# Three pairs of feed-forward groups as seven block products each, in a two-block transformer kernel

## The chip, the core and the metric

The kernel runs on one core of a Trainium2 chip as a single launch. The metric is the device time of that launch in microseconds (us); smaller is better. TensorE is called PE in the rows, VectorE DVE, ScalarE ACT, GpSimd POOL and SyncE SP; PEld is TensorE's loading of the stationary operand.

## What is computed

Two blocks of two layers each run over 256 tokens of width 1024. Every layer has a feed-forward, a token mixer and a second feed-forward, so there are eight feed-forwards, and the change touches these alone. Cut to what matters:

```python
D_MODEL, SEQ, D_FF = 1024, 256, 2816

def swiglu(x, w13, w2):                      # first block
    a, b = jnp.split(x @ w13, 2, axis=-1)    # w13: 1024 x 5632
    return (jax.nn.silu(a) * b) @ w2         # w2: 2816 x 1024

x = layer_norm(ALPHA * x + 0.5 * swiglu(x, ffn1_w13[l], ffn1_w2[l]), ln_g[l, 0], ln_b[l, 0])
m = mixer(x, ...)
x = layer_norm(ALPHA * x + m, ln_g[l, 1], ln_b[l, 1])
x = layer_norm(ALPHA * x + 0.5 * swiglu(x, ffn2_w13[l], ffn2_w2[l]), ln_g[l, 2], ln_b[l, 2])
# second block: the same swiglu with rms_norm around it, x = x + 0.5 * rms_norm(h, gain)
```

All of it is float32. A product of two float32 matrices is made of three TensorE products in a reduced type: each operand is split into a high part (a rounding copy) and a low part (the difference), and high times high, high times low and low times high are summed in PSUM.

## The kernel before

The tokens are two halves of 128 rows, i = 0 and 1. Weights come in units of 128x1024 float32 (512 KB), one DMA each, in the exact order in which they are used (the host lays them out so; `fetch`, line 215, issues on SP's queue into `stg`, 4 buffers). `split` (line 257) makes of each unit the high part `wh` on ScalarE (line 267) and the low part `wl` on VectorE (line 273), in two halves of 512 columns. `wh` and `wl` are tiles of one ring, `whp`, of 24 tiles, so 12 split units at most stand ahead of TensorE. All other work tiles of 128x512 float32 (activations, normalisation rows, hidden parts) share one pool `sp` of 31 slots.

A feed-forward (`ffn`, line 376) has 66 units: 11 groups of 4 units for the first product and 22 rows of one unit for the second. A group `g` is 256 columns of the gate and 256 of the up part; for each token half it is 24 matmuls of 128x128 by 128x512 into one PSUM bank of the pool `grp` (4 banks). `hidden` (line 395) takes the bank: Silu on ScalarE, product on VectorE, then two clock steps later two transposes on TensorE and a high and a low part `hT`. A row is 12 matmuls for both halves into the accumulators `accs` (pool `big`, 4 banks). The first two groups (`OWN`) run by each token half on its own, since the halves arrive at different times from the layer before; then `joint` (line 417) runs both halves on each unit, in the order of the tuple `FFN` (line 57); the last six rows run by each half again.

The order of work is set in two ways. `run_all` writes the program with a counted clock (`later(n, fn)` puts `fn` n steps on, a joint unit counts two steps), and SP and POOL run exactly in that order. TensorE, VectorE and ScalarE are put in order by a planner, which plays the program through with its own costs, takes ready instructions by program order, and hands out ring tiles and slots as they come free in its plan; on the chip each engine then runs that fixed list. `mm3` (line 297, matmuls on line 301) is the helper behind nearly all matmuls, `transposed` (line 282, line 285) the one behind all transposes. `to_x` (line 303) turns the layer's input into `xh` and `xl`, the stationary parts of the next feed-forward or mixer.

In four of the eight feed-forwards POOL multiplies norm gains in advance: `pre_gains` (line 451, 4 operations) in the second feed-forward of the first block's second layer, and `gains` (line 510, 6 operations) in three of the second block's four. They use rows that SP loads in the middle of the weight stream (`prepare`, line 361).

Before the change the tuple `FFN` has no entry of kind "s", so `made` is None for every unit, and `operand` and the lists of products stand unused.

## Time and profile before

| | us |
|---|---|
| median of 3 runs | 2211.48 (2207.61 to 2212.41) |
| the profiled execution | 2206.83 |
| its span in the trace | 2205.1 |
| TensorE busy | 2169.9 (98% of the span) |
| VectorE busy | 1456.1 (66%) |
| ScalarE busy | 1173.5 (53%) |
| GpSimd busy | 271.5 (12%) |
| granted TensorE clock | 0.997 of full speed |

The span is the profiled execution without some 1.7 us around it. Matmuls overlap: one shows 0.39 us, but they follow each other at a shorter pitch, so the pitch is read from runs of many, not from the mean of one. The same holds for VectorE and ScalarE back to back.

### The profile page before, as it was taken

Reading aid. Unit: us, or ns where it says so; the run is one execution under the profiler, and the core shown is the slowest. Engines: PE = TensorE matmul, PEld = TensorE weight load, DVE = VectorE, ACT = ScalarE, POOL = GpSimd, SP = SyncE. Lnnn points to the kernel's source line nnn. Section 1 sums busy time; section 2 is a strip of 40 time slices with the busy share of each in tenths; the row PEclk is TensorE's granted clock in tenths of the full one; section 3 lists DMA queues with packets and bytes.
Section 4 is the critical chain, followed back from the end, with each engine's and each line's share of the span. In section 5 each row is a group of like instructions: output and inputs, shape, how many; then the busy total and the mean of one; then the engine's idle time right before and its main releaser. Section 6 shows DMA issues by size and latency. Waiting matters only on the chain.

```text
span 2205.1 us, 29139 instructions
## 1 busy us (share of the span) xinstructions
PE 2169.9 (98%) x10256; PEld 1791.8 (81%) x10256; DVE 1456.1 (66%) x2653; ACT 1173.5 (53%) x2339; POOL 271.5 (12%) x319
## 2 busy tenths in 40 slices
PE   8999999999999999999999999999999999999998
PEld 6888888888888888888878887788888888788887
DVE  6656787655755679666584668676657466877463
ACT  6544755544544475554554554665446355566352
POOL 0000420000000033001001004610100100650000
PEclk9999999999999999999999999999999999999999
DMA  7855455655565445565645643537555474345561
GB/s 275 271 189 158 148 182 175 223 196 189 182 205 188 156 158 181 180 203 191 210 157 196 218 145 120 172 102 238 182 190 177 157 236 149 114 134 167 177 219 49
DMA packets 115299, 394.59 MB, mean 179 GB/s; under 512 B 12880, under 2 KB 15312, under 8 KB 115152
## 3 DMA queue, kind: packets, MB, share of 16 engines
q1 hardware_dynamic: 115152, 392.73, 53.8%
q8 instruction: 80, 1.31, 0.2%
q14 instruction: 67, 0.55, 0.1%
HBM read 391.63 MB, written 1.05 MB: 178 GB/s over the span
## 4 chain that ended last, share of the span: by engine, by line
PE 88%; DVE 5%; ACT 2%; DMA 2%; POOL 2%; issue 1%; SPq 0%; DVEq 0%; POOLq 0%; ACTq 0%
PE g L301 54%; PE big L301 26%; PE g L285 3%; DMA stg<-in_ws_dram 2%; DVE wl L273 2%; ACT wh L267 1%; PE big L1150 1%; PE big L1179 1%; PE big L680 1%; DVE x L481 0%; DVE t L480 0%; PE big L1097 0%; POOL cu L1023 0%; PE big L882 0%; POOL qk L1024 0%
## 5 line engine op out<-in xcount | busy, mean ns | idle before, releaser
L273 DVE TENSOR_TENSOR wl<-stg,wh 128x512 fp32r<-128x512 f32 x1410 | 952.0, 708 | 506.7 <-ACT wh L267 498.5
L267 ACT ACTIVATE wh<-stg 128x512 fp32r<-128x512 f32 x1424 | 831.5, 625 | 622.7 <-PE g L301 313.6
L301 PE MATMUL g<-wh,xh 128*128 128x512 f32 x1952 | 783.0, 401 | 11.5 <-ACT wh L267 6.9
L301 PE MATMUL g<-wl,xh 128*128 128x512 f32 x1952 | 763.5, 391 | 0.0
L301 PE MATMUL g<-wh,xl 128*128 128x512 f32 x1952 | 762.6, 392 | 0.0
L301 PEld LDWEIGHTS g<-wh,xh 128*128 128x128 f32 x1952 | 368.4, 189 | 89.1 <-ACT xh L308 8.1
L301 PEld LDWEIGHTS g<-wh,xl 128*128 128x128 f32 x1952 | 367.9, 188 | 80.2 <-DVE xl L309 1.4
L301 PEld LDWEIGHTS g<-wl,xh 128*128 128x128 f32 x1952 | 368.6, 189 | 70.9 <-DVE wl L273 0.4
L301 PE MATMUL big<-wh,hT 128*128 128x512 f32 x1408 | 392.1, 391 | 0.0
L301 PEld LDWEIGHTS big<-wh,hT 128*128 128x128 f32 x1408 | 262.6, 188 | 53.6
L301 PE MATMUL big<-wl,hT 128*128 128x512 f32 x704 | 222.3, 390 | 0.0
L301 PEld LDWEIGHTS big<-wl,hT 128*128 128x128 f32 x704 | 132.2, 188 | 27.9
L373 POOL TENSOR_TENSOR m<-m,nhalf 128x1 f32<-128x1 f32 (+1 forms) x24 | 23.1, 964 | 848.3 <-DVE m L372 848.3
L507 POOL TENSOR_TENSOR m<-m,nhalf 128x1 f32<-128x1 f32 x24 | 15.3, 638 | 639.6 <-DVE m L506 639.6
L411 DVE TENSOR_TENSOR hT<-g,hT 128x256 fp32r<-128x256 f32 x176 | 68.2, 419 | 32.6 <-ACT hT L410 32.5
L410 ACT ACTIVATE hT<-g 128x256 fp32r<-128x256 f32 x176 | 59.3, 375 | 54.3 <-PE g L285 53.9
L400 ACT ACTIVATE sg<-g,m 128x256 f32<-128x256 f32 x88 | 41.0, 466 | 87.2 <-PE g L301 87.0
L405 DVE TENSOR_TENSOR sg<-g,sg 128x256 f32<-128x256 f32 x88 | 37.1, 421 | 69.1 <-ACT sg L400 67.0
L400 ACT ACTIVATE sg<-g 128x256 f32<-128x256 f32 x88 | 33.2, 377 | 54.9 <-PE g L301 54.9
L285 PE MATMUL g<-con,sg 128*128 128x128 f32 x352 | 57.4, 273 | 3.4 <-DVE sg L405 2.0
L285 PEld LDWEIGHTS g<-con,sg 128*128 128x128 f32 x352 | 43.7, 140 | 20.6 <-PE g L285 3.7
L402 DVE SCALAR_TENSOR_TENSOR sg<-g,sg 128x256 f32<-128x256 f32 x88 | 37.1, 421 | 30.2 <-ACT sg L400 28.9
(273 smaller groups left out, 1669.6 us busy)
## 6 DMA issues: line engine op xcount, KB each, us to landing
stg<-in_ws_dram SPq DMA_DIRECT2D x711, 512.0 KB, 4.0
row<-in_norm_gain_dram SPq DMA_DIRECT2D x24, 256.0 KB, 5.5
row<-in_ln_g_dram SPq DMA_DIRECT2D x12, 256.0 KB, 5.2
row<-in_ln_b_dram SPq DMA_DIRECT2D x12, 256.0 KB, 6.4
xT<-in_xT_dram SPq DMA_DIRECT2D x4, 256.0 KB, 6.4
x<-in_x_dram SPq DMA_DIRECT2D x4, 256.0 KB, 5.8
out_dram<-x SPq DMA_DIRECT2D x4, 256.0 KB, 2.0
con<-in_con_dram SPq DMA_DIRECT2D x1, 528.0 KB, 6.1
```

Of the source, the lines that this page charges most:

```text
L267: r = self.nc.scalar.activation(hi[:, c], w[:, c], AF.Copy)
L273: self.nc.vector.tensor_sub(lo[:, c], w[:, c], hi[:, c])
L285: self.nc.tensor.transpose(tp[:, hs(j)], src[:, hs(j)], self.ident)
L301: self.nc.tensor.matmul(accs[c], a, b[c], start=start and q == 0, stop=stop and q == 2)
L373: self.nc.gpsimd.tensor_tensor(out, out, self.nhalf[:, 0:n], op=ALU.pow)
L400: nc.scalar.activation(sg[:, 0:256], acc[:, 0:256], AF.Silu, scale=1.0 if rs is None else rs)
L402: nc.vector.scalar_tensor_tensor(sg[:, 256:512], acc[:, 256:512], 0.5, sg[:, 0:256], op0=ALU.mult, op1=ALU.mult)
L405: nc.vector.tensor_mul(sg[:, 256:512], acc[:, 256:512], sg[:, 0:256])
L410: nc.scalar.activation(t[:, 0:256], tp[:, 0:256], AF.Copy)
L411: nc.vector.tensor_sub(t[:, 256:512], tp[:, 0:256], t[:, 0:256])
L680: nc.tensor.matmul(ps[:, 64 * h:64 * h + 64].rearrange("p (c m) -> p c m", m=m), Z[:, hs(h)], view(Z[:, hs(h)], m)[:, :, 1, :], start=True ...
L1150: nc.tensor.matmul(ps[:, hh * S + j * P:hh * S + j * P + P], J["aq", i][r, hs(head // 2)], J["ak", j][r, hs(head // 2)], start=True, stop= ...
```

## The change

In each feed-forward three pairs of neighbouring groups (2 and 3, 4 and 5, 6 and 7) are computed in another way. A pair is a product of X (256 tokens by 1024) with W (1024 by 512 gate and 512 up columns), taken as 2 by 2 blocks: token halves by halves of the inner dimension, and halves of the inner dimension by gate or up. The eight block products become seven (Strassen's scheme in its form with 15 sums, the signs put into the X sums). A block product is 12 matmuls of 512 columns.

- `sums` makes four sums of X blocks on VectorE and splits them (four high copies on ScalarE, four differences on VectorE); for that `to_x` keeps float32 copies `A` of the transposed input by four more ScalarE copies per feed-forward. The parts take eight slots until the last pair is done.
- The four W blocks are loaded as before, 8 units per pair, but into tiles of the ring `whp`. Three products use them as they are in part: p1, p2, q5 and p3 each have a load of their own; q5, p6, p7 and q4 are made by one `tensor_add` of 128x1024 on VectorE per unit, in place. All 14 units of a pair are split, each by one ScalarE copy and one VectorE difference of 128x1024.
- `pair` runs the products in PSUM: p1, p6, p7 and q4 accumulate in one bank, and `keep` copies the bank out by ScalarE after p1, p6 and p7; q5 and p3 share another, copied after q5; p2 has a third. Three `tensor_add` and two products on VectorE and two Silu on ScalarE make the two hidden parts of 512 columns, each transposed by four transposes.
- The order: two own groups, then group 8, pair 2, group 9, pair 4, group 10, pair 6, rows 8, 9, 20, 21, and the last six rows 10 to 15. Inside a pair one row of the second product stands after p1, q5, p6 and p7. A feed-forward has 84 split units from the same 66 loads.

```diff
-FFN = (("g", 2), ("g", 3), ("r", 0, 8), ("g", 4), ("g", 5), ("g", 6), ("g", 7), ("r", 8, 16),
-       ("g", 8), ("g", 9), ("g", 10))
-LAST = (16, 17, 18, 19, 20, 21)
-PRODUCTS = ("p1", "q5", "p6", "p3", "p7", "p2", "q4")
-NEEDS = dict(p1="11", q5="12", p6="22", p2="21")
+FFN = (("g", 8), ("s", 2, 0, 1, 2, 3), ("g", 9), ("s", 4, 16, 17, 4, 5), ("g", 10), ("s", 6, 6, 7, 18, 19),
+       ("r", 8), ("r", 9), ("r", 20), ("r", 21))
+LAST = (10, 11, 12, 13, 14, 15)
+PRODUCTS = ("p1", "p2", "q5", "p3", "p6", "p7", "q4")
+LOADS = dict(p1="11", p2="21", q5="12", p3="22")
+BLOCKS = ("11", "21", "12", "22")
+GAPS = ("p1", "q5", "p6", "p7")
...
     def fetch(self, v):
         while self.next_dma <= min(v, self.nunit - 1):
             made = self.made[self.next_dma]
-            if made is None:
+            if not self.product(self.next_dma):
                 t = self.stages[self.next_dma] = self.stg.tile([P, 1024], F32, tag="stg", name=self.nm("stg"))
-            elif made[0] in NEEDS:
-                t = self.raw[NEEDS[made[0]], made[1]] = self.whp.tile([P, 1024], F32, tag="w", name=self.nm("raw"))
-            else:
-                t = None
-            if t is not None:
-                for c in (slice(0, 512), slice(512, 1024)) if self.next_raw == 0 else (slice(0, 1024),):
-                    self.nc.sync.dma_start(t[:, c], self.a["ws"][self.next_raw][:, c])
-                self.next_raw += 1
+                for c in (slice(0, 512), slice(512, 1024)) if self.next_dma == 0 else (slice(0, 1024),):
+                    self.nc.sync.dma_start(t[:, c], self.a["ws"][made][:, c])
+            elif made[0] in LOADS:
+                t = self.raw[made[:2]] = self.whp.tile([P, 1024], F32, tag="w", name=self.nm("raw"))
+                self.nc.sync.dma_start(t, self.block(LOADS[made[0]], *made[1:]))
             self.next_dma += 1
...
+    def block(self, b, u, base):
+        return self.a["ws"][base + 2 * BLOCKS.index(b) + u]
+    def operand(self, p, u, base):
 
 
         raw, add = self.raw, self.nc.vector.tensor_add
-        if p == "p1":
-            return raw["11", u]
-        if p == "q5":
-            t = raw.pop(("11", u))
-            add(t, t, raw["12", u])
-            raw["t1", u] = t
+        if p in ("q5", "p6"):
+            t = raw["p1", u]
+            add(t, t, raw["q5" if p == "q5" else "p3", u])
             return t
-        if p == "p6":
-            t = raw["t2", u] = self.whp.tile([P, 1024], F32, tag="w", name=self.nm("sum"))
-            add(t, raw.pop(("t1", u)), raw["22", u])
+        if p == "p7":
+            t = raw.pop(("p3", u))
+            add(t, t, raw.pop(("q5", u)))
             return t
-        if p == "p3":
-            return raw["22", u]
-        if p == "p7":
-            t = raw.pop(("12", u))
-            add(t, t, raw.pop(("22", u)))
+        if p == "q4":
+            t = raw.pop(("p1", u))
+            add(t, t, raw.pop(("p2", u)))
             return t
-        if p == "p2":
-            return raw["21", u]
-        t = raw.pop(("t2", u))
-        add(t, t, raw.pop(("21", u)))
-        return t
+        return raw[p, u]
...
-            w = self.stages.pop(v) if made is None else self.operand(*made)
+            product = self.product(v)
+            w = self.operand(*made) if product else self.stages.pop(v)
             hi = self.whp.tile([P, 1024], F32R, tag="w", name=self.nm("wh"))
             lo = self.whp.tile([P, 1024], F32R, tag="w", name=self.nm("wl"))
             halves = [slice(0, 512), slice(512, 1024)]
-            for h, c in enumerate(halves if made is None else [slice(0, 1024)]):
+            for h, c in enumerate([slice(0, 1024)] if product else halves):
...
-    def to_x(self, i, srcs):
-
+    def to_x(self, i, srcs, keep=False):
+        tps = []
         for h, src in enumerate(srcs):
             tp = self.transposed(src)
             hi, lo = (t[:, i, 512 * h:512 * h + 512] for t in (self.xh, self.xl))
             self.nc.scalar.activation(hi, tp, AF.Copy)
             self.nc.vector.tensor_sub(lo, tp, hi)
+            tps.append(tp)
+        if keep:
+            for h, tp in enumerate(tps):
+                t = self.sh["A", i, h] = self.slot(name="A")
+                self.nc.scalar.activation(t, tp, AF.Copy)
...
+    def sums(self, X):
+        nc = self.nc
+        for p, i, h in (("p1", 0, 0), ("p2", 0, 1), ("q4", 1, 1)):
+            X[p] = tuple(t[:, i, 512 * h:512 * h + 512] for t in (self.xh, self.xl))
+        a11, a12, a21, a22 = (self.sh.pop(("A", i, h)) for i in range(2) for h in range(2))
+        minus = lambda t, a, b: nc.vector.scalar_tensor_tensor(t, a, -1.0, b, op0=ALU.mult, op1=ALU.subtract)
+        def parts(p, t):
+            hi, lo = self.slot((P, 512), F32R, "Xh"), self.slot((P, 512), F32R, "Xl")
+            nc.scalar.activation(hi, t, AF.Copy)
+            nc.vector.tensor_sub(lo, t, hi)
+            X[p] = hi, lo
+        nc.vector.tensor_sub(a22, a22, a21)
+        nc.vector.tensor_sub(a21, a11, a21)
+        yield 1
+        parts("q5", a22)
+        yield 1
+        minus(a11, a22, a11)
+        yield 1
+        minus(a12, a11, a12)
+        yield 1
+        parts("p3", a12)
+        yield 1
+        parts("p6", a11)
+        yield 1
+        parts("p7", a21)
...
+        if i == 1:
+            J["X"] = {}
+            self.later(2, lambda: self.start(self.sums(J["X"])))
...
+        for what, n, *ks in FFN:
+            if what == "s":
+                yield from self.pair(J, n, ks)
...
+    def on(self, J, k):
+        wh, wl = self.units[self.pos[1]]
+        for i in range(2):
+            xh, xl = J["h", i, k]
+            self.mm3(J["accs", i], xh, xl, wh, wl, k == 0, False)
+        self.both(1)
+        yield
+    def pair(self, J, g, ks):
+        nc = self.nc
+        first = dict(p1="p1", p2="p2", q5="q5", p3="q5", p6="p1", p7="p1", q4="p1")
+        bank, kept, sg = {}, {}, {}
+        rows = dict(zip(GAPS[len(GAPS) - len(ks):], ks))
+        def keep(p):
+            t = kept[p] = self.slot(name="k" + p)
+            nc.scalar.activation(t, bank[p], AF.Copy)
+        def add(t, other):
+            nc.vector.tensor_add(t, t, other)
+        def silu(out, src, i):
+            rs = J["rs", i]
+            nc.scalar.activation(out, src, AF.Silu, scale=1.0 if rs is None else rs)
+        def hidden(i, t, sg):
+            nc.vector.scalar_tensor_tensor(t, t, -0.5 if J["rs", i] is None else -1.0, sg,
+                                           op0=ALU.mult, op1=ALU.mult)
+            def turn():
+                hi, lo = self.to_T(t, "hT")
+                for c in range(4):
+                    J["h", i, 2 * g + c] = hi[:, hs(c)], lo[:, hs(c)]
+            self.later(2, turn)
+        def after(p):
+            if p in ("p1", "q5", "p6", "p7"):
+                keep(p)
+            if p == "p2":
+                t = sg[0] = kept.pop("p1")
+                add(t, bank[p])
+                silu(t, t, 0)
+            elif p == "p6":
+                t = kept.pop("p6")
+                add(t, bank["p3"])
+                hidden(0, t, sg.pop(0))
+            elif p == "p7":
+                add(kept["p7"], kept.pop("q5"))
+            elif p == "q4":
+                t = self.slot(name="sg")
+                silu(t, bank[p], 1)
+                hidden(1, kept.pop("p7"), t)
+        for p in PRODUCTS:
+            bank[p] = self.bank(self.grp, "g") if first[p] == p else bank[first[p]]
+            xh, xl = J["X"][p]
+            for u in range(2):
+                wh, wl = self.units[self.pos[1]]
+                for j in range(2):
+                    k = 2 * u + j
+                    for q, (x, w) in enumerate(((xh, wh), (xh, wl), (xl, wh))):
+                        nc.tensor.matmul(bank[p], x[:, hs(k)], w[j], start=first[p] == p and k + q == 0,
+                                         stop=k == 3 and q == 2, skip_group_check=True)
+                for i in range(2):
+                    self.pos[i] += 1
+                if u:
+                    after(p)
+                yield
+            if p in rows:
+                yield from self.on(J, rows[p])
...
+    out, n = list(range(4 * OWN)), 4 * OWN
+    for what, _, *ks in FFN:
         if what == "s":
-            out += [(p, u) for p in PRODUCTS for u in range(2)]
+            base, gaps = n, GAPS[len(GAPS) - len(ks):]
+            n += 8
+            for p in PRODUCTS:
+                out += [(p, u, base) for u in range(2)]
+                if p in gaps:
+                    out.append(n)
+                    n += 1
         else:
-            out += [None] * (4 if what == "g" else at[1] - at[0])
-    return out + [None] * len(LAST)
+            m = 4 if what == "g" else 1
+            out += range(n, n + m)
+            n += m
+    return out + list(range(n, n + len(LAST)))
```

## Rows read from the trace of the kernel before

**Rows 1.** Page, busy time: engine, us, share of span, instructions.

```profile
span 2205.1 us, 29139 instructions
...
PE 2169.9 (98%) x10256; PEld 1791.8 (81%) x10256; DVE 1456.1 (66%) x2653; ACT 1173.5 (53%) x2339; POOL 271.5 (12%) x319
```

**Rows 2.** Chain that ended last, 460 to 520 us: start, length, what, count.

```profile
464.49 10.94 PE g L301 x48
475.43 0.44 PE g L285 x4
...
498.62 19.09 PE big L301 x84
```

**Rows 3.** Groups by line and shape, whole span: busy us, mean ns, idle before.

```profile
L273 DVE TENSOR_TENSOR wl<-stg,wh 128x512 fp32r<-128x512 f32 x1410 | 952.0, 708 | 506.7 <-ACT wh L267 498.5 <-PE g L285 3.4 <-PE g L301 0.7
...
L411 DVE TENSOR_TENSOR hT<-g,hT 128x256 fp32r<-128x256 f32 x176 | 68.2, 419 | 32.6 <-ACT hT L410 32.5
...
L471 DVE SCALAR_TENSOR_TENSOR t<-x,big 128x512 f32<-128x512 f32 x24 | 16.1, 683 | 15.8 <-PE big L301 15.8
...
L827 DVE TENSOR_TENSOR y<-y,y 128x512 f32<-128x512 f32 x8 | 5.5, 689 | 0.1
...
L813 ACT ACTIVATE b<-g 128x512 f32<-128x512 f32 x8 | 4.7, 591 | 2.2 <-PE g L301 2.2
```

**Rows 4.** Timeline, VectorE and ScalarE runs back to back: start, length, instruction, count.

```profile
14.28 5.13 DVE L273 TENSOR_TENSOR wl<-stg,wh 128x512 fp32r<-128x512 f32 x8 [0.17 <-ACT wh L267]
...
51.26 3.69 DVE L273 TENSOR_TENSOR wl<-stg,wh 128x512 fp32r<-128x512 f32 x6
...
1559.25 0.76 DVE L411 TENSOR_TENSOR hT<-g,hT 128x256 fp32r<-128x256 f32 x2 [2.43 <-ACT hT L410]
...
25.78 2.72 ACT L267 ACTIVATE wh<-stg 128x512 fp32r<-128x512 f32 x5
...
1558.83 0.66 ACT L410 ACTIVATE hT<-g 128x256 fp32r<-128x256 f32 x2 [2.46 <-PE g L285]
```

**Rows 5.** Waits, whole span: who for whom, us in total, times, longest.

```profile
DVE wl L273 <- ACT wh L267: 498.5, 422, 4.0
ACT wh L267 <- PE g L301: 313.6, 269, 2.8
...
POOL gr L458 <- PE big L301: 61.3, 1, 61.3
```

**Rows 6.** Windows: stretch, length, busy PE, PEld, DVE, ACT, POOL, clock, DMA share, GB/s.

```profile
381.00:409.00 28.00, 27.50 (x127) 22.31 (x128) 23.92 (x44) 17.23 (x34) 1.00 (x1) 1.00 0.60 203
...
1524.00:1545.00 21.00, 21.00 (x96) 17.39 (x95) 11.74 (x18) 9.10 (x18) 2.60 (x2) 1.00 0.68 233
1545.00:1568.00 23.00, 23.00 (x105) 19.00 (x104) 8.12 (x11) 4.93 (x12) 6.73 (x5) 1.00 0.14 46
1568.00:1592.00 24.00, 24.00 (x111) 19.86 (x110) 19.57 (x36) 17.31 (x35) 0.00 (x0) 1.00 0.84 283
```

**Rows 7.** Timeline, 1540 to 1556 us: POOL, VectorE, ScalarE around the gains.

```profile
1542.40 1.29 POOL L519 TENSOR_TENSOR xg<-x,row 128x512 f32<-128x512 f32 x1 [53.58 <-PE big L301]
...
1548.75 2.99 POOL L519 TENSOR_TENSOR xg<-x,row 128x512 f32<-128x512 f32 x2
...
1542.50 6.83 DVE L273 TENSOR_TENSOR wl<-stg,wh 128x512 fp32r<-128x512 f32 x4 [1.43 <-ACT wh L267]
...
1554.53 0.47 ACT L400 ACTIVATE sg<-g,m 128x256 f32<-128x256 f32 x1 [8.82 <-PE g L301]
```

**Rows 8.** Line 267 from 0 to 1544.97 and to 1567.6 us: high halves begun (xN).

```profile
L267 ACT ACTIVATE wh<-stg x1027: 612/630/657, 4.7 to 1544.6; 128x512 fp32r<-128x512 f32 x172
...
L267 ACT ACTIVATE wh<-stg x1031: 612/629/657, 4.7 to 1566.8; 128x512 fp32r<-128x512 f32 x172
```

**Rows 9.** Chain that ended last, whole span: end of eight rows, start of group 4.

```profile
1544.97 13.60 PE g L301 x60
```

More of the change, by code (lines that the diff above doesn't have):

```diff
@@ L95, in __init__ @@
         self.phase, self.made = [], []
-        ffn = _ffn_units()
+        at = 0
         for what, _ in order:
             mixer = ("mixer1", 56) if what == "b1" else ("mixer2", 36)
-            for kind, made in (("ffn", ffn), (mixer[0], [None] * mixer[1]), ("ffn", ffn)):
+            for kind, made in (("ffn", _ffn_units()), (mixer[0], list(range(mixer[1]))), ("ffn", _ffn_units())):
                 self.phase += [(kind, m) for m in range(len(made))]
-                self.made += made
+                self.made += [m + at if isinstance(m, int) else (*m[:2], m[2] + at) for m in made]
+                at += FFN_ROWS if kind == "ffn" else len(made)
         self.nunit = len(self.made)
-        self.raw, self.next_raw = {}, 0
+        self.raw = {}
         self.next_dma = self.next_split = 0
@@ L432, in joint @@
                         for i in range(2):
[L433 removed]
+                            self.hidden(J, i, acc[i], n)
                     yield
             else:
[L436 to L442 removed]
@@ L560, in rms @@
         yield NORM
[L561 removed]
+        self.to_x(i, xg, spread)
         rs2 = self.small(1)
@@ L1375, in _ffn @@
     parts = [groups[:4 * OWN]]
-    for what, *at in FFN:
+    for what, n, *ks in FFN:
         if what == "s":
-            parts.append(_blocks(w_in, *at))
+            parts += [_blocks(w_in, n), w_out[list(ks)]]
         else:
-            parts.append(groups[4 * at[0]:4 * at[0] + 4] if what == "g" else w_out[at[0]:at[1]])
+            parts.append(groups[4 * n:4 * n + 4] if what == "g" else w_out[n:n + 1])
     return parts + [w_out[list(LAST)]]
```

36 lines of the change are left out of this document (13 added, 23 removed).

## Prediction

> **What bounds the kernel now.** I read the busy times first. TensorE is busy 2169.9 of 2205.1 us and VectorE 1456.1 [rows 1]. A busy TensorE can still be waiting inside, so I went on to the chain that ended last. In the joint part of a feed-forward it lies on TensorE without a break: 48 matmuls in 10.94 us, 84 in 19.09 us, four transposes in 0.44 us [rows 2]. That is 0.2273 us a matmul and 0.11 us a transpose, and the reader is to see that nothing else stands between. Third, the waits: VectorE's split waits for ScalarE's (498.5 us in total) and ScalarE's for TensorE (313.6 us over the groups alone) [rows 5], so the ring of 24 tiles is full and both run as far ahead as it lets them. Line 267 shows how far: by 1544.97 us, when TensorE ends the eighth row of the sixth feed-forward [rows 9], 1027 high halves have begun [rows 8], which is 513.5 units. By the code TensorE has then done 502 (478 before this feed-forward, 8 own, two groups, eight rows), so 11.5 units or some 31 us of TensorE's work lie ready. The kernel is bound by the number of matmuls, and every other engine has slack, spread unevenly.
>
> **What the change takes away.** A pair is now 7 products of 12 matmuls, 84 instead of 96. Transposes stay at 8 per pair (two halves by four), rows and groups elsewhere are the same. So 12 x 0.2273 = 2.73 us less per pair, and 24 pairs make 65.5 us [rows 2]. A gain beyond that is excluded: no idle time of TensorE lies in the stretches that change (the windows from 1524 to 1592 us are busy in full [rows 6]).
>
> **What it adds, on VectorE.** Back to back, six differences of 512 columns took 3.69 us and one takes 0.69, so the pitch is (3.69 - 0.69)/5 = 0.60; eight took 5.13, pitch 0.634. Two of 256 columns took 0.76 with 0.42 for one, pitch 0.34 [rows 3, 4]. The slope is 0.26 us per 256 columns, so 1024 columns cost an estimated 0.60 + 0.52 = 1.12; the upper bound is two of 512 at 0.634, 1.27. A sum of two SBUF tiles costs what a difference does (689 ns against 708 at 512 columns), one with a PSUM operand 683 [rows 3], so I price the sums as differences.
> One pair: 14 splits and 8 block sums of 1024, 22 x 1.12 = 24.6; the four rows between, 8 x 0.60 = 4.8; three sums, two products, two differences on the results, 7 x 0.64 = 4.5. Together 33.9 us (upper 37.8). TensorE needs (84 + 48) x 0.2273 + 8 x 0.11 = 30.9. Inside a pair VectorE is the slower one, by 3.0 us (upper 6.9).
> The single group ahead: 8 x 0.60 + 4 x 0.34 = 6.2 on VectorE against 48 x 0.2273 + 0.44 = 11.4 on TensorE. Group and pair together are 40.1 us (upper 44.6) of VectorE in 42.3 us of TensorE.
> One feed-forward: splits +18.2 (42 units at 1.20 and 42 at 1.12 against 66 at 1.20), block sums 24 x 1.12 = 26.9, X sums and parts 8 x 0.60 = 4.8, results +5.2. That is +55 us, eight times 440, so VectorE goes from 1456 to some 1896 us, 87% of the new time.
>
> **What hides it.** The lead. The eight raw tiles of a pair sit in the ring, so 16 tiles or 8 split units are left; a pair's 18 units (14 halves of products, 4 rows) average 30.9/18 = 1.72 us, so the lead in a pair is 7 to 8 units, some 12 us, not 31. Three rounds lose 3 us in each pair and win back up to 5 in each group, and 12 us covers that. With the upper prices a round loses 2.2 us net, and three still fit. If VectorE waits for ScalarE a tenth of the time, 4 us more per round, the lead is gone at the end of the third. The stall per pair is therefore between 0 and 2.2 us; I take 0.4, near the bottom because the cover is there in most rounds: 24 x 0.4 = 10 us.
> ScalarE: five copies took 2.72 us, two of 256 columns 0.66 [rows 4], hence 0.52 per 512 and 1.0 per 1024 columns; 14 x 1.0, 8 x 0.52 for the rows and 8 evictions, Silus and high parts at 0.59 [rows 3] are 22.9 us of 30.9. It is not the bound.
> The handovers in PSUM: p3, p7 and q4 write a bank that ScalarE must first copy out. The copy takes 0.59 [rows 3], behind at most one running 1.0, and the row between is 12 x 0.2273 = 2.73. Nothing, as long as ScalarE's list holds no late operand in front of the copy.
> Loads: bytes are the same, 16 loads per round or 198 GB/s, but 10 of them fall on the first 16.4 us of a pair, 320 GB/s, where catching up showed 283 [rows 6]. `stg` and the early raw tiles cover it.
> Entry of a feed-forward: VectorE is busy 23.9 of 28 us already [rows 6], and 4.8 us of X sums and four copies on ScalarE come on top. They are needed only at q5, one group and three products' time later, and slide into the single group. Between 0 and 1 us per feed-forward; I take 0.25, 2 us in all.
>
> **The gains on POOL.** This is the largest term. In the sixth feed-forward POOL works from 1542.40 to 1551.74 us, and four differences beside it take 6.83 us [rows 7] where four back to back would take 0.69 + 3 x 0.60 = 2.5 [rows 4], 4.3 us lost. But the order made it worse: after them ScalarE stands 8.82 us before a Silu that waits for TensorE [rows 7], VectorE is busy 8.12 of 23 us and the loads fall to 46 GB/s [rows 6]. By 1567.6 us only 1031 halves have begun [rows 8], 515.5 units against 510 done: the lead fell by 6 units, 6 x 2.73 = 16 us of TensorE's work. TensorE did not notice, since 31 us were there. In a pair 12 us are there, and catching up needs a VectorE with time to spare, which the pair rounds do not have. Four feed-forwards hold such an event. Loss 4.3 to 16 against a lead of 7 to 12: stall between 0 and 9 each; I take 5, near the middle, since the order is planned anew and part of the 16 was lead that could be spent at no price. 4 x 5 = 20 us.
> The Trainium skill, SBUF — State Buffer, section Who interferes with whom, says that a `tensor_tensor` with both inputs in SBUF contends with GpSimd's reads and that the loser fully blocks for the whole instruction. The 4.3 us agree in kind; by the rule taken to its end all of POOL's 9.3 us would be lost, and the sum below would be 2198.
>
> **The sum.** The profiled execution took 2206.8 us (span 2205.1). 2206.8 - 65.5 + 10 + 2 + 20 = 2173.3. The median of the runs lies 4.7 us above that execution, so 2178.
>
> **The rivals.**
> *VectorE keeps the lead everywhere*, the gains too, and only the count of matmuls decides: 2211.5 - 65.5 and a few us, 2150. For it: 87% mean load and a TensorE without a break today. Against: the fall of the lead at 1545 us. Chance 0.26.
> *POOL's gains block VectorE in full* through the wide sums: each event loses 9.3 instead of 4.3 us with the lead already spent, 4 x 5 = 20 more, 2198. Chance 0.09.
> *Slots run out.* At the head of the third pair I count 4 residuals, 8 X parts, 12 hidden parts, 8 rows and gains and 2 kept banks, 34 for 31 slots, where gains are made. Before, POOL already waited 61.3 us for a slot [rows 5]. A hidden part would wait until the second row of the pair frees four; 4 us four times, 2194. Chance 0.05.
> *Late evictions.* If ScalarE's list puts the copy behind an operand that is late, each of three handovers per pair costs about 0.6 us: 72 x 0.6 = 43 in place of the 10 for the pairs, 2211.5 - 65.5 + 43 + 22 = 2211, no change. Chance 0.04.
> *Slower: VectorE sets the pace of the whole round.* Its 40.1 us of work in a round stretch with each wait for ScalarE or a load. The change gains 2.73 us a round and the lead lends 12/3 = 4, so it loses from a round of 42.3 + 2.7 + 4 = 49 us, that is when VectorE is busy less than 0.82 of the time. While catching up it reached 19.57 of 24, just 0.82 [rows 6], but with loads as the limit there; at the entry 0.85. At 0.80 a round is 50.1, 3.8 beyond cover, 24 x 3.8 = 91: 2206.8 - 65.5 + 91 + 4.7 = 2237. Chance 0.16.
>
> **How the numbers follow.** My forecast, 2178 with its own range 2160 to 2195, has 0.40. The range 2147 to 2222 takes in the clean case, the blocked gains, the slots and the late evictions, and leaves out most of the slower case and the lucky end. Some 0.2% is what a measurement of this kernel can tell from no change (4.4 us, about its spread of runs). Faster: 0.40 + 0.26 + 0.09 + 0.05 and a little, less the tails, 0.77; same 0.07 (late evictions and the upper tail of the forecast); slower 0.16.
>
> **What would show it.** TensorE has 288 matmuls fewer at the same 0.227 us. VectorE is busy near 1900 us. In feed-forwards without gains the chain stays on TensorE through all three pairs; in the four with gains it leaves TensorE after the event, for VectorE's sums and splits, some 5 us each. A 1024-column difference shows a pitch near 1.12. If the chain runs over VectorE in most pairs, my lead is wrong and the slower case holds; if it never leaves TensorE, the gains cost nothing; if it waits for evictions in front of p3, p7 or q4, the rows between are too short a cover.

## The result and the profile after

| | before | after |
|---|---|---|
| median of four runs each, us | 2210.47 | 2170.01 |
| lowest to highest, us | 2207.61 to 2212.41 | 2169.18 to 2171.18 |
| profiled execution, us | 2206.83 | 2170.61 |
| its span, us | 2205.1 | 2168.8 |

The ratio of the runs is 0.9818, with a 95% interval of 0.9801 to 0.9835. The kernel became faster by 40.5 us, and its time lies 8 us below the forecast of 2178.

First the busy times of the page, as in [rows 1] (engine, us, share of the span, instructions):

```profile
span 2168.8 us, 28670 instructions
...
PE 2116.2 (98%) x9968; PEld 1738.6 (80%) x9968; DVE 1879.8 (87%) x2837; ACT 1352.0 (62%) x2351; POOL 291.4 (13%) x319
```

TensorE has 288 matmuls fewer, VectorE 424 us more to do. Then the costliest groups by line and shape, the answer to [rows 3] (busy us, mean ns, idle before; line 274 makes the low half of a weight, 268 the high half, 245, 249 and 253 the sums of blocks):

```profile
L274 DVE TENSOR_TENSOR wl<-stg,wh 128x512 fp32r<-128x512 f32 x1026 | 691.8, 708 | 129.6 <-ACT wh L268 123.3 <-PE g L286 3.4 <-PE big L302 1.1
...
L274 DVE TENSOR_TENSOR wl<-raw,wh 128x1024 fp32r<-128x1024 f32 x336 | 410.2, 1236 | 25.1 <-ACT wh L268 23.1
L268 ACT ACTIVATE wh<-raw 128x1024 fp32r<-128x1024 f32 x336 | 349.3, 1056 | 178.1 <-DVE raw L253 53.7 <-DVE raw L245 50.7 <-DVE raw L249 25.3
...
L245 DVE TENSOR_TENSOR raw<-raw,raw 128x1024 f32<-128x1024 f32 x96 | 120.6, 1268 | 0.5
```

The idle time in these rows tells who waits now: ahead of its copies of the products' operands ScalarE stands 178.1 us, at least 129.7 of them (53.7 + 50.7 + 25.3) for VectorE's sums. The waits over the whole span say the same, and the slack of [rows 5] has shrunk from 498.5 us to 146.4 for VectorE and from 313.6 to 107.3 for ScalarE behind the groups:

```profile
DVE wl L274 <- ACT wh L268: 146.4, 159, 3.4
...
ACT wh L268 <- PE g L302: 107.3, 92, 4.1
```

Third, the chain that ended last from 460 to 520 us, the second feed-forward, where no gains are made (start, length, what):

```profile
475.73 2.72 PE big L302 x12
478.45 2.50 PE g L547 x11
480.95 0.44 PE g L286 x4
481.39 0.23 PE g L547
481.62 2.75 PE big L302 x12
484.37 2.72 PE g L547 x12
```

The products are line 547. As in [rows 2], 12 matmuls take 2.72 us and nothing stands between them. The windows of the same feed-forward (us, then busy PE, PEld, DVE, ACT, POOL, granted clock, DMA share, GB/s; first pair, single group, second pair, single group, third pair) show how near VectorE is to the limit:

```profile
413.60:444.50 30.90, 30.88 (x141) 25.34 (x140) 27.43 (x35) 19.46 (x31) 0.00 (x0) 1.00 0.59 209
444.50:456.00 11.50, 11.50 (x54) 9.52 (x53) 9.06 (x11) 7.16 (x10) 0.00 (x0) 1.00 0.79 282
456.00:487.00 31.00, 31.00 (x142) 25.62 (x141) 30.83 (x38) 20.58 (x33) 0.00 (x0) 1.00 0.38 137
487.00:498.00 11.00, 11.00 (x52) 9.11 (x51) 10.61 (x13) 7.53 (x11) 0.00 (x0) 1.00 0.97 357
498.00:529.00 31.00, 31.00 (x143) 25.62 (x142) 30.35 (x39) 20.65 (x32) 0.00 (x0) 1.00 0.31 106
```

TensorE never stops, though VectorE is busy 30.8 of 31 us.

**Where the time went.** I took from the matmul records, for each feed-forward, the time from the first matmul of the joint part to the first one behind it (624 matmuls before, 588 after). A joint part that kept all of its 36 x 0.2273 would be 8.18 us shorter.

| feed-forward | 1 | 2 | 3 | 4 | 5 | 6 | 7 | 8 | sum |
|---|---|---|---|---|---|---|---|---|---|
| before, us | 145.76 | 146.32 | 145.69 | 146.18 | 145.68 | 146.61 | 146.72 | 145.69 | 1168.7 |
| after, us | 140.56 | 138.18 | 138.16 | 140.99 | 142.21 | 141.95 | 142.70 | 138.22 | 1123.0 |
| given back of 8.18 | 2.98 | 0.04 | 0.65 | 2.99 | 4.71 | 3.52 | 4.16 | 0.71 | 19.8 |

Of 65.5 us removed the joint parts kept 45.7. Gains are made in feed-forwards four to seven, and these give back 15.4 of the 19.8. All stretches outside the joint parts together became 9.5 us longer, 11.3 of it in the stretches ahead of the first five joint parts and the rest slightly negative. 65.5 - 19.8 - 9.5 = 36.2, the difference of the spans (36.3).

**The gains.** Timeline of POOL and VectorE in the sixth feed-forward (start, length, instruction, and in brackets the idle time before with its releaser); it answers to [rows 7]:

```profile
1548.07 8.08 POOL L633 TENSOR_TENSOR gg<-row,row 128x512 f32<-128x512 f32 x1 [7.39 <-PE big L302]
1556.12 1.30 POOL L631 TENSOR_TENSOR xg<-x,row 128x512 f32<-128x512 f32 x1
1560.43 1.62 POOL L633 TENSOR_TENSOR gg<-row,row 128x512 f32<-128x512 f32 x1 [3.02 <-issue]
...
1549.17 2.35 DVE L274 TENSOR_TENSOR wl<-raw,wh 128x1024 fp32r<-128x1024 f32 x2
...
1556.20 2.29 DVE L274 TENSOR_TENSOR wl<-raw,wh 128x1024 fp32r<-128x1024 f32 x1 [1.21 <-ACT wh L268]
...
1560.21 2.98 DVE L274 TENSOR_TENSOR wl<-stg,wh 128x512 fp32r<-128x512 f32 x3
```

POOL's product at 1548.07 lasts 8.08 us, while VectorE's queue beside it runs at its usual pace (two of 1024 columns in 2.35). It ends at 1556.15, at the end of the 1.21 us that VectorE stood still ahead of 1556.20. Then it is VectorE's turn to lose: 2.29 us for an instruction of 1.22. TensorE's next wait is in its own timeline:

```profile
1558.26 0.39 PE L547 MATMUL g<-wl,Xh 128*128 128x512 f32 x1
1560.44 0.63 PE L286 MATMUL g<-con,kp 128*128 128x128 f32 x4 [1.80 <-DVE kp L511]
```

It doesn't wait for a weight. It waits to transpose a hidden part, whose product (line 511) stands in VectorE's queue behind the lengthened split. The other three feed-forwards with gains show the same. TensorE's waits over the whole span (who for whom, us in total, times, longest):

```profile
PE g L286 <- DVE kp L511: 7.3, 6, 1.8
PE g L286 <- DVE sg L445: 4.8, 7, 0.9
PE g L547 <- ACT kp L501: 2.5, 2, 1.4
PE g L302 <- DVE wl L274: 0.5, 1, 0.5
```

Line 445 is the product that makes a hidden part of a single group. All six waits for line 511 and six of the seven for line 445 lie in the joint parts four to seven, 11.1 us of the 15.4 given back there. No wait for a split lies in them; the only one for a low half (0.5 us) is in the first.

**The exits.** After the third feed-forward's rows, TensorE's timeline and the windows around it:

```profile
740.57 0.66 PE L286 MATMUL g<-con,x 128*128 128x128 f32 x4 [1.40 <-DVE x L593]
742.59 0.63 PE L286 MATMUL g<-con,x 128*128 128x128 f32 x4 [1.36 <-DVE x L593]
...
740.00:743.00 3.00, 1.07 (x9) 0.86 (x9) 3.00 (x6) 0.60 (x1) 0.00 (x0) 1.00 0.84 264
743.00:747.00 4.00, 4.00 (x13) 3.13 (x12) 3.76 (x8) 2.67 (x5) 0.00 (x0) 0.57 0.33 124
```

The layer norm is short work on VectorE, but VectorE is still refilling the ring, puts splits between its steps and is busy all of the 3.00 us. The chain that ended last has such a split between two steps of the norm (lines 592 and 593):

```profile
740.52 0.66 DVE t L592
741.18 0.60 DVE wl L274
741.78 0.67 DVE x L593
```

TensorE is busy 1.07 of the 3.00 us, and then its granted clock falls: 0.57 over the next 4 us (part of it at the lower level, 1.2 GHz), worth (1 - 0.57) x 4 = 1.7 us. A like pair of windows stands at the exit of the fourth feed-forward (1111.5 us, 0.57 over 4 us). Summed over the span, TensorE lost 6.7 us of full-speed time to a lower clock before and 11.4 after.

### The profile page after: what moved, and what is told of

Same layout as the page of the kernel before. It is cut to its first block, busy times and chain, and to the rows that moved or that the text cites. A ratio compares the mean times of both kernels' runs of the same rounds, so it can differ in the third digit from the quotient of the medians.

```text
span 2168.8 us, 28670 instructions
## 1 busy us (share of the span) xinstructions
PE 2116.2 (98%) x9968; PEld 1738.6 (80%) x9968; DVE 1879.8 (87%) x2837; ACT 1352.0 (62%) x2351; POOL 291.4 (13%) x319
## 4 chain that ended last, share of the span: by engine, by line
PE 80%; DVE 10%; issue 3%; ACT 3%; POOL 2%; DMA 2%; SPq 0%; DVEq 0%; POOLq 0%; ACTq 0%
PE g L302 33%; PE big L302 23%; PE g L547 17%; DVE wl L274 5%; PE g L286 4%; ACT wh L268 2%; DMA stg<-in_ws_dram 2%; PE big L1262 1%; PE big L1291 1%; PE big L792 1%; DVE raw L245 1%; DVE kp L504 0%; DVE raw L249 0%; PE big L1209 0%; POOL cu L1135 0%
## 5 line engine op out<-in xcount | busy, mean ns | idle before, releaser
L274 DVE TENSOR_TENSOR wl<-stg,wh 128x512 fp32r<-128x512 f32 x1026 | 691.8, 708 | 129.6 <-ACT wh L268 123.3
L268 ACT ACTIVATE wh<-stg 128x512 fp32r<-128x512 f32 x1040 | 600.8, 623 | 200.8 <-PE g L302 83.8
L302 PE MATMUL g<-wh,xh 128*128 128x512 f32 x1184 | 483.1, 408 | 9.3 <-ACT wh L268 5.9
L302 PE MATMUL g<-wl,xh 128*128 128x512 f32 x1184 | 467.2, 395 | 0.5 <-DVE wl L274 0.5
L302 PE MATMUL g<-wh,xl 128*128 128x512 f32 x1184 | 465.3, 395 | 0.0
L268 ACT ACTIVATE wh<-raw 128x1024 fp32r<-128x1024 f32 x336 | 349.3, 1056 | 178.1 <-DVE raw L253 53.7
L274 DVE TENSOR_TENSOR wl<-raw,wh 128x1024 fp32r<-128x1024 f32 x336 | 410.2, 1236 | 25.1 <-ACT wh L268 23.1
L302 PE MATMUL big<-wh,hT 128*128 128x512 f32 x640 | 183.3, 390 | 0.0
L547 PE MATMUL g<-wh,Xh 128*128 128x512 f32 x384 | 149.7, 390 | 1.1 <-ACT kp L501 1.1
L547 PE MATMUL g<-wl,Xh 128*128 128x512 f32 x384 | 150.7, 393 | 0.0
L547 PE MATMUL g<-wh,Xl 128*128 128x512 f32 x384 | 150.2, 391 | 0.0
L302 PEld LDWEIGHTS big<-wh,hT 128*128 128x128 f32 x640 | 120.1, 188 | 25.3
L547 PE MATMUL g<-wh,xh 128*128 128x512 f32 x288 | 114.6, 398 | 1.4 <-ACT kp L501 1.4
L547 PE MATMUL g<-wl,xh 128*128 128x512 f32 x288 | 112.5, 391 | 0.0
```

The source lines that it names most:

```text
L268: r = self.nc.scalar.activation(hi[:, c], w[:, c], AF.Copy)
L274: self.nc.vector.tensor_sub(lo[:, c], w[:, c], hi[:, c])
L302: self.nc.tensor.matmul(accs[c], a, b[c], start=start and q == 0, stop=stop and q == 2)
L547: nc.tensor.matmul(bank[p], x[:, hs(k)], w[j], start=first[p] == p and k + q == 0, stop=k == 3 and q == 2, skip_group_check=True)
```

## The experiments

The first four kernels ran together, then the next four, then the last two; the kernel before took 2211.1, 2210.1 and 2209.9 us beside them. The joint parts and what the stretches outside gained or lost against the kernel before, in the profiled executions (the last column is the full-speed time lost to a lower clock):

| kernel | joint parts 1 to 8, us | sum | outside | clock |
|---|---|---|---|---|
| after | 140.6 138.2 138.2 141.0 142.2 142.0 142.7 138.2 | 1123.0 | +9.5 | 11.4 |
| e1_gains_memset | 140.5 138.2 138.2 138.2 138.4 138.2 138.3 138.5 | 1108.3 | +8.6 | 10.9 |
| e3_groups_first | 142.8 144.4 142.8 151.6 149.7 151.4 149.7 139.7 | 1172.0 | +11.9 | 26.8 |
| e4_group_behind | 139.8 138.7 138.1 143.6 146.4 146.2 142.5 140.1 | 1135.3 | +0.6 | 13.2 |
| e5_rows_behind | 152.2 145.9 144.9 146.7 145.9 145.9 148.6 140.9 | 1171.0 | +7.3 | 15.6 |
| e6_no_block_sums | 139.1 138.2 138.2 139.2 140.3 139.9 139.9 138.5 | 1113.2 | -1.0 | 9.1 |
| e7_one_pair | 144.2 144.6 143.6 143.6 143.9 144.0 143.9 144.3 | 1152.1 | +3.2 | 9.9 |
| e8_gains_vector | 140.5 138.2 138.2 138.2 138.4 138.3 138.2 138.2 | 1108.1 | +15.3 | 9.4 |
| e9_behind_gains_vector | 140.2 138.8 138.6 138.1 139.7 138.7 139.0 138.8 | 1111.8 | +5.6 | 10.0 |
| e10_behind_in_block1 | 139.7 139.1 138.1 138.2 138.4 138.2 138.2 138.2 | 1108.0 | +6.8 | 11.5 |
| e11_groups_first_no_sums | 138.3 138.3 138.3 140.0 140.0 140.0 140.3 138.4 | 1113.5 | +0.1 | 8.0 |

**POOL's reads or the slots?** The edit, in each of the three lines that make gains (one is shown):

```diff
-            pool.tensor_tensor(xg[h], self.x[i][h], gp[h], op=ALU.mult)
+            pool.memset(xg[h], 1.0)
```

> The changed kernel with POOL's gain products left out: the ten tiles that they make per layer pair are filled with constants by POOL instead, so POOL writes them and reads nothing. Slots, rows and order stay. If POOL's reads beside VectorE are what the four feed-forwards with gains lose (their joint parts take 141.0, 142.2, 142.0 and 142.7 us, the later three without gains 138.2), all come to about 138.2 and the time falls by some 15 us to 2155. If the shortage of slots is the cause, they stay near 142 and the time at 2170.

Measured: 2156.83 us, ratio 0.9756 (0.974 to 0.9772). Joint parts four to seven come to 138.2 to 138.4, the length of those that never had gains; the slots are taken as before. The slots are refuted, POOL's work beside VectorE is shown. VectorE's timeline at the place shown above, where POOL now does nothing, and ahead of it one of POOL's memsets with VectorE's instructions beside it:

```profile
1546.51 1.22 DVE L274 TENSOR_TENSOR wl<-raw,wh 128x1024 fp32r<-128x1024 f32 x1 [1.21 <-ACT wh L268]
...
1549.45 1.89 DVE L274 TENSOR_TENSOR wl<-stg,wh 128x512 fp32r<-128x512 f32 x3
...
1539.27 0.53 POOL L633 MEMSET gg<- 128x512 f32 x1 [7.97 <-PE big L302]
...
1539.47 2.36 DVE L274 TENSOR_TENSOR wl<-raw,wh 128x1024 fp32r<-128x1024 f32 x2
```

1.22 and 1.89 stand where 2.29 and 2.98 stood: 1.1 us each. Beside the memset two instructions of 1024 columns take 2.36 together, their usual pace. The Trainium skill, SBUF — State Buffer, section Who interferes with whom, says that a VectorE instruction with two SBUF inputs contends with a GpSimd instruction that reads SBUF, not with one that only writes it. These rows agree, the 2.36 us beside the memset with the second half.

**The single groups: first, or behind.** The raw tiles are also named by their pair, since pairs now follow each other; for the rest the edit is the order:

```diff
-FFN = (("g", 8), ("s", 2, 0, 1, 2, 3), ("g", 9), ("s", 4, 16, 17, 4, 5), ("g", 10), ("s", 6, 6, 7, 18, 19),
+FFN = (("g", 8), ("g", 9), ("g", 10), ("s", 2, 0, 1, 2, 3), ("s", 4, 16, 17, 4, 5), ("s", 6, 6, 7, 18, 19),
```

> The same work with the three single groups ahead of all three pairs, which then run back to back. By the account of the lead (VectorE 33.9 us of work in 30.9 us of TensorE per pair, some 12 us of lead), three pairs in a row use up 9 us of it: 0 to 3 us lost per feed-forward, some 8 to 10 where gains fall in, 2170 to 2200, likeliest 2185. If the place of the groups does not matter, 2170. If there is no lead worth the name and VectorE sets the pace of a pair, 3 us per pair are lost, 24 x 3 = 72, 2240.

Measured: 2221.36 us, ratio 1.0043 (1.0028 to 1.0058), slower than the kernel before and outside what was expected. To see why I counted the lead from the records: the units whose low half VectorE has finished less those that TensorE has begun, in TensorE's time. In the second feed-forward:

| at the head of | joint part | first pair | second pair | third pair | lowest |
|---|---|---|---|---|---|
| after, us of work | 13.6 | 10.9 | 8.2 | 8.2 | 4.1 |
| e3_groups_first | 19.1 | 9.5 | 5.5 | 0 | 0 |

In the changed kernel the groups between the pairs keep the lead level. In a row, two pairs use it up, and the third runs at VectorE's and ScalarE's pace. In the feed-forwards with gains TensorE then stood up to 4 us at once, and its clock fell behind that. The windows at the fourth feed-forward:

```profile
1068.00:1074.50 6.50, 2.83 (x13) 2.00 (x11) 6.45 (x7) 3.39 (x5) 0.00 (x0) 1.00 0.59 228
1074.50:1078.00 3.50, 3.42 (x7) 2.06 (x7) 3.50 (x5) 1.89 (x3) 0.00 (x0) 0.51 0.16 28
```

TensorE is busy 2.83 of 6.50 us, VectorE 6.45, and the granted clock of the next 3.5 us is 0.51, the lower level. Over the span this kernel lost 26.8 us of full-speed time, 15 more than the changed kernel; that is at most what the clock has of the 51 us between them, for in part of it TensorE stood anyway.

The other order, a group behind each pair:

```diff
-FFN = (("g", 8), ("s", 2, 0, 1, 2, 3), ("g", 9), ("s", 4, 16, 17, 4, 5), ("g", 10), ("s", 6, 6, 7, 18, 19),
+FFN = (("s", 2, 0, 1, 2, 3), ("g", 8), ("s", 4, 16, 17, 4, 5), ("g", 9), ("s", 6, 6, 7, 18, 19), ("g", 10),
```

> The same work with each single group behind its pair instead of ahead. The stretches outside the joint parts lost 9.5 us in all, most where a layer norm of the first block follows the last rows. If that comes from VectorE still refilling the ring behind the third pair, a group behind it gives 5 us to refill and these losses fall to some 3 us; the first pair starts with a lead built in the own groups alone and may lose 0 to 3 us: 2160 to 2180, likeliest 2167. If the losses there have another cause, they stay, and the first pair's start decides: 2170 to 2190.

Measured: 2173.37 us, ratio 0.9826 (0.9811 to 0.984). The stretches outside lose 0.6 us in place of 9.5: with a group behind the last pair, VectorE has refilled the ring by the layer norm. That confirms the cause of the exits. But joint parts four to seven give back another 10.8 us. The waits of TensorE in the fifth feed-forward (1130 to 1280 us) are for results again, as at 1560 us in the changed kernel:

```profile
PE g L286 <- DVE kp L511: 3.7, 3, 1.9
```

Three falls of the clock in these four parts (at 1023, 1245 and 1583 us, 3.4 us each) are worth another 5. Why gains cost more in this order was not settled; a later run shows that they do so only as POOL's work.

**Are the evictions or VectorE covered by the rows between?**

```diff
-FFN = (("g", 8), ("s", 2, 0, 1, 2, 3), ("g", 9), ("s", 4, 16, 17, 4, 5), ("g", 10), ("s", 6, 6, 7, 18, 19),
+FFN = (("g", 8), ("s", 2), ("r", 0), ("r", 1), ("r", 2), ("r", 3), ("g", 9), ("s", 4), ("r", 16), ("r", 17),
+       ("r", 4), ("r", 5), ("g", 10), ("s", 6), ("r", 6), ("r", 7), ("r", 18), ("r", 19),
```

> The same work with the four rows of a pair behind it instead of between the products. If the rows hide the copies out of PSUM, p3, p7 and q4 now wait for a copy of 0.59 us and some 0.3 us of handing over, 72 x 0.9 = 65 us, and VectorE falls behind inside the bare pair (29 us of work in 20) beyond the lead: 2235 or more. If the copies were hidden anyway, since TensorE has other work to put there, 2170 to 2180.

Measured: 2216.18 us, ratio 1.0016 (1.0005 to 1.0026): the whole gain is gone, and the time lies between the two expectations. The chain that ended last, in its second pair (start, length, what; the lines have one number more here), names one reason:

```profile
476.19 1.14 DVE raw L246
477.33 1.14 DVE wl L275
478.46 1.13 DVE raw L250
479.60 1.14 DVE wl L275
...
487.55 0.59 DVE kp L505
```

The chain is VectorE's, instruction behind instruction at 1.13 to 1.14 us, with an eviction's sum (0.59) among them. Without rows the products ask VectorE for 33.9 - 4.8 = 29.1 us in 84 x 0.2273 + 0.9 = 20 us. From 468 to 491 us TensorE was busy 19.99 of 23. The evictions are the other reason. TensorE's waits over the whole span have

```profile
PE g L548 <- ACT kp L502: 13.1, 20, 0.7
PE g L548 <- ACT kq L502: 3.8, 8, 0.5
```

or 16.9 us in 28 waits for copies out of PSUM, where the changed kernel has 2.5 us in two. So the rows do both: they cover evictions and they spread VectorE's work. The joint parts grew by 48.0 us; the waits for copies are about a third of that, and how the rest divides was not settled. The first expectation had both mechanisms and put the evictions (65 us) far too high.

**VectorE's load.** The sums of weight blocks are left out, and everything else stays:

```diff
-            add(t, t, raw["q5" if p == "q5" else "p3", u])
...
-            add(t, t, raw.pop(("q5", u)))
+            raw.pop(("q5", u))
...
-            add(t, t, raw.pop(("p2", u)))
+            raw.pop(("p2", u))
```

> Left out: the 24 sums of weight blocks per feed-forward (192 in all); the four products that would read a sum read a loaded block, so the outputs are other numbers. Loads, tiles, splits and TensorE's work stay. VectorE has 192 x 1.13 = 217 us less to do, 9 us per pair (33.9 becomes 24.9, under TensorE's 30.9). Theory (what is given back is VectorE's: it still refills the ring at the layer norms after a feed-forward, +9.5 us, and POOL's gains slow it where it has no room, 15.4 us): the stretches outside the joint parts lose under 2 us against the kernel before, joints four to seven come near 138.2, and the time is about 2148 (2143 to 2156). Rival (the exits lose to the new order of rows and loads, the gains to the slots): 2165 to 2171, VectorE merely idles more.

Measured: 2150.93 us, ratio 0.9729 (0.9714 to 0.9743), the loads and buffers being the same. The stretches outside win 1.0 us, so the exits' loss is VectorE's. Joint parts four to seven come to 139.2 to 140.3: with room on VectorE those with gains lie 1.0 to 2.1 us above 138.2 instead of 2.8 to 4.5. The page's busy line gives the size, 1879.8 less 1671.2 or 208.6 us for 192 sums, 1.09 each:

```profile
PE 2108.2 (98%) x9968; PEld 1735.1 (81%) x9968; DVE 1671.2 (78%) x2645; ACT 1360.4 (63%) x2351; POOL 277.6 (13%) x319
```

The same in the order that had been slower than the kernel before, to settle that miss:

> The three single groups first and then the three pairs in a row (2221 us), and the 24 sums of weight blocks per feed-forward left out, so the outputs are other numbers. Theory (three pairs in a row ask VectorE for 3 x 33.9 us in 92.7 us of TensorE's, and what it is behind at the third pair is TensorE's to wait): without the sums a pair asks 24.9 us, and the time falls to where leaving out the sums put the kernel with single groups between the pairs, 2148 to 2160. Rival (the order itself, through the loads or the buffers that the pairs hold at once): 2190 or more.

Measured: 2152.75 us, ratio 0.9744 (0.9727 to 0.976), 68.6 us less than with the sums. The order costs nothing by itself; VectorE, with no group between the pairs, is what it cost. For that order the cause is settled but for one point: leaving the sums out also takes away ScalarE's waits for them. That VectorE was busy 6.45 of 6.50 us where TensorE stood speaks for its load.

**One pair instead of three.**

```diff
-       ("g", 9), ("s", 4, 16, 17, 4, 5), ("g", 10), ("s", 6, 6, 7, 18, 19),
+       ("g", 9), ("r", 16), ("r", 17), ("g", 4), ("g", 5), ("r", 4), ("r", 5),
+       ("g", 10), ("r", 6), ("r", 7), ("g", 6), ("g", 7), ("r", 18), ("r", 19),
```

> One pair of groups per feed-forward by products (the one behind the first single group), the other four groups plain, rows between them: 8 x 12 x 0.2273 = 21.8 us of matmuls removed against the kernel before instead of 65.5. If what is given back grows with the pairs (the changed kernel kept 40.5 of 65.5, 62%): 2211 - 13.5 = 2197. If it comes from VectorE's backlog, which one pair early in the joint part (33.9 us of VectorE in 30.9) can't leave behind for the gains or the exit: nearly all of 21.8 is kept, 2189 to 2191. Likeliest 2190.

Measured: 2194.42 us, ratio 0.9927 (0.9911 to 0.9944): 15.7 us of 21.8 kept, between the two figures and nearer to the one I thought less likely. Gains cost nothing here (143.9 in the joint parts with them, 143.6 to 144.6 in those without), as the backlog would have it, but each joint part lies some 0.6 us above 146.1 - 2.7 and the stretches outside lose 3.2. Where those come from I didn't settle.

**Gains on VectorE.**

```diff
-                    self.nc.gpsimd.tensor_tensor(t[h], self.sh[(n,) + ln][h], gp[h], op=ALU.mult)
+                    self.nc.vector.tensor_tensor(t[h], self.sh[(n,) + ln][h], gp[h], op=ALU.mult)
...
-        pool = self.nc.gpsimd
+        pool = self.nc.vector
```

> The gain products (six 128x512 per feed-forward in feed-forwards four to seven) move from POOL to VectorE at the same places, nothing left out. Theory (POOL reading beside VectorE costs VectorE 1 to 4 us for each of them): on VectorE they cost 6 x 0.6 = 3.6 us of its time, joints four to seven come to 138.2 to 140, the time to 2157 to 2164, likeliest 2160. Rival (VectorE has no room in the pairs, so each us added to it is a us of the end): 15.4 us lost become 4 x 3.6 = 14.4, the time stays at 2169.

Measured: 2163.7 us, ratio 0.9789 (0.9773 to 0.9806); its runs spread from 2161.51 to 2168.52, so the step from the changed kernel's 0.9818 is read from the joint parts. Four to seven fall to 138.2 to 138.4, 14.8 us less in all. Six instructions of 0.68 us (four in the fourth feed-forward) on a full VectorE cost TensorE next to nothing there. So it was not that VectorE had no room at all; it had no room to be held up. The last two of the six:

```profile
1565.64 0.68 DVE L631 TENSOR_TENSOR xg<-x,row 128x512 f32<-128x512 f32 x1
1567.38 0.68 DVE L631 TENSOR_TENSOR xg<-x,row 128x512 f32<-128x512 f32 x1
```

But the stretches outside lose 15.3 instead of 9.5, and a part of the gain came back there.

**Both at once, and then sorted by block.**

> Single group behind each pair (exits lost 0.6 us there instead of 9.5) and the gain products on VectorE: both changes at once. Theory, if the two losses are apart: 2173.4 - (143.6 + 146.4 + 146.2 + 142.5 - 4 x 139) = 2150.7; 2146 to 2158. Rival (VectorE, fuller at the end of such a joint part, is late whoever does the gains): 2165 to 2173.

Measured: 2156.17 us, ratio 0.9753 (0.9739 to 0.9768): groups behind the pairs and VectorE's gains go together, and joint parts four to seven take 138.1 to 139.7 where POOL's gains made them 142.5 to 146.4. But the stretches outside lose 5.6 us where 0.6 was expected. The last kernel takes each order where it lost least (`FFN_B2` is the changed kernel's order):

```diff
+FFN = dict(b2=FFN_B2, b1=(("s", 2, 0, 1, 2, 3), ("g", 8), ("s", 4, 16, 17, 4, 5), ("g", 9),
+                          ("s", 6, 6, 7, 18, 19), ("g", 10), ("r", 8), ("r", 9), ("r", 20), ("r", 21)))
...
-        for what, n, *ks in FFN:
+        for what, n, *ks in FFN["b1" if rs is None else "b2"]:
...
-                        self.later(n + 12, lambda: self.gains(i, post, pre))
+                        self.later(n + 12, lambda: self.gains(i, post, pre, nc.gpsimd if n == 40 else nc.vector))
```

> Nothing left out. In the four feed-forwards of the first block the single groups stand behind their pairs, in the four of the second block ahead of them; the gain products that fall into a joint part are VectorE's, those that fall into a mixer stay POOL's. If the losses are apart and lie where the runs so far put them: joint parts one to four as with groups behind and VectorE's gains (140.2, 138.8, 138.6, 138.1), five to eight as with groups ahead and VectorE's gains (138.4, 138.3, 138.2, 138.2), so 1108.5 for 1123.0 in the changed kernel; outside them -0.2, 0.1, 0.2, 0.6, -0.1 and from the sixth on as in the changed kernel, -1.3 in all for +9.5. Span 2143.5, time about 2145.5 (2143 to 2150). Rival (what a feed-forward leaves to do comes up at the next place whatever the order): no better than with groups behind everywhere, 2154 to 2160.

Measured: 2152.86 us, ratio 0.9743 (0.9728 to 0.9757), the fastest that computes everything, 17 us below the changed kernel and 57 below the kernel before. It lies above the 2143 to 2150 that was expected. The joint parts came out as expected (1108.0), the outside did not: +6.8 for -1.3, nearly all of it (7.7 of 8.1) ahead of the joint parts five to eight, where now the feed-forwards' exits lose. The windows at the last of them, ahead of the eighth feed-forward:

```profile
1804.00:1807.50 3.50, 1.57 (x7) 0.86 (x6) 3.50 (x7) 3.47 (x11) 0.00 (x0) 1.00 0.26 76
1807.50:1811.00 3.50, 3.50 (x9) 2.73 (x10) 3.50 (x8) 1.12 (x3) 0.74 (x2) 0.52 0.19 76
```

VectorE is busy throughout, TensorE 1.57 of 3.50, and the clock behind it is 0.52: (1 - 0.52) x 3.5 = 1.7 of the 2.9 us lost in that stretch. So the rival was partly right: time that the gains had cost inside a joint part came up at the exit behind it. The gains of the mixers are not at fault there: ahead of the eighth joint part the loss is 2.9 us with them on POOL, and was 2.5 and 3.4 in the two kernels that had them on VectorE. Ahead of the sixth they may have a part: 0.9 us with them on POOL, 2.9 on VectorE with the same order in the second block. Why the exits of the second block lose once the joint parts don't was not settled further.

## Why the prediction was right, and where its steps were not

The forecast of 2178 lies 8 us above the result, and the likeliest case was the one that came. In terms of the profiled execution the sum said 2173.3, and that execution took 2170.61. The rest is the 4.7 us that I added because the median lay so far above the profiled execution of before; after, the median (2170.0) lies 0.6 below it. That difference belonged to one execution, not to the kernel.

- *288 matmuls, 65.5 us.* Right: 10256 against 9968, 2.72 us for 12 in the chain.
- *VectorE's prices.* 1.12 us for 1024 columns; the rows show 1.13 to 1.14. Its total was to be 1896, it is 1879.8. Its load in a pair was 33.9 for TensorE's 30.9; the windows show it busy 30.83 of 31, which says that it was full and not how much it was asked for.
- *The lead.* 12 us at a pair: counted from the records, 10.9 us at the first, 8.2 at the others, lowest 4.1 in the second feed-forward. That it lasts for three rounds is right, and a group between the pairs is a condition for it: with the groups first it was gone by the third pair, and 51 us with it; with each group behind its pair the first three feed-forwards, which make no gains, lost little (139.8, 138.7, 138.1).
- *Pairs without gains, 10 us.* Over-sized. Feed-forwards one, two, three and eight gave back 4.4 together, 3.0 of it in the first. There one wait is a late eviction, in TensorE's timeline:

```profile
118.42 0.50 PE L547 MATMUL g<-wh,xh 128*128 128x512 f32 x1 [1.42 <-ACT kp L501]
```

ScalarE's copy of the bank stood behind the copy of a weight, which is the mechanism of the fourth rival. I saw it twice in 72 handovers (the other 1.07 us, in the seventh feed-forward).

- *The gains, 20 us.* The place, the cause and roughly the size were right: 15.4. The mechanism was wrong. I let the weight lead be spent, so that TensorE would wait for sums and splits. In the four feed-forwards the lead never fell below 2.7, 6.8, 5.5 and 5.5 us of work, and no wait for a split lies in them. What was late were results, 11.1 us of waits: in the sixth the product on line 511, with a transpose due soon behind it, in a queue of 1.2 us instructions where one took 2.29. A lead in weights doesn't cover that. The rival that blocked gains cost 9.3 us each has fallen, though POOL was the one that stood longest (8.08 us); VectorE lost 1.1 us at a time. The Trainium skill, SBUF — State Buffer, section Who interferes with whom, calls the contention an exclusive lock. These rows agree: against a queue without gaps POOL was the loser, and it lost for as long as the queue had none.
- *Entries, 2 us.* The step that failed most. I looked at what a feed-forward's entry adds on VectorE (4.8 us) and not at what its joint part leaves behind. The stretches outside lost 9.5 us, by the exits and layer norms of the first block, where VectorE still refilled the ring, 3.4 of it through the clock that fell behind two such stalls. Leaving out the sums, or a group behind the last pair, takes it away (-1.0 and +0.6).
- *The slower case* didn't occur here. It is real, one edit away: without rows between the products, or without groups between the pairs, the gain is gone (2216 and 2221 us). The condition that I gave for it, a VectorE busy less than 0.82 of the time, is not what brought it about: it was busy 21.77 of 23 us (468 to 491) in the one and 6.45 of 6.50 in the other. The order of the work made the full VectorE late, in the first with exposed evictions beside it.
- *The lead kept everywhere, 2150* and *slots run out, 2194* are settled: the first did not come, though with the gains or VectorE's load out of the way the kernel takes 2151 to 2157; and with the slots as they are the gains' loss goes away.

The errors were of both signs: 5.6 and 4.6 us too much for pairs and gains, 7.5 too little outside, and 4.7 for the median. That they left only 8 us is in part luck.

## What to carry to other kernels

When an edit trades matmuls for work on an engine that had slack, count that engine stage by stage and then follow its backlog to the next serial place, here a layer norm, where the bound engine has nothing else to run. Spread the new work between stages that leave the engine free: the same instructions in another order were worth 50 us here. A lead in one operand covers that operand alone; for results that the bound engine needs back soon, ask what is queued in front of them, and move an engine that fights for the same reads out of those stages, even onto the busy engine itself.

## What was not expected of the hardware

- POOL's product of two 512-column tiles took 1.30 us at 1556.12 and 8.08 ahead of that, beside a queue of VectorE's without gaps; VectorE lost 1.1 us where it was held up. Beside a memset of such a tile (0.53 us) two of VectorE's instructions kept their pace (2.36 us).
- TensorE's granted clock fell to the lower level for some 3.5 us behind stalls as short as these: busy 1.07 of 3.00 us, then 0.57 over 4 us; 1.57 of 3.50, then 0.52 over 3.5. Each such fall was worth 1.7 us on top of the stall, and not each stall had one: the 1.80 us at 1560 us did not (granted clock 1.00 on both sides). The kernel with its groups first lost 15 us more than the changed kernel in this way.
